# Expert weights in 8 KB pieces per partition, tokens transposed by strided reads, and padded tile addresses

## The chip, the core and the metric

The kernel runs on one core of a Trainium2 chip. Its metric is device time in microseconds (us), from the first to the last instruction, including what the launch adds. The engines are TensorE (PE, with its weight loads shown apart as PEld), VectorE (DVE), ScalarE (ACT), GpSimd (POOL) and SyncE (SP, which here issues nearly all loads). SBUF has 128 partitions; a tile is a number of bytes at the same address in every partition.

## What is computed

Two transformer blocks follow one another on 1024 tokens of 1024 features, all in float32. The first mixes tokens with a gated short convolution, the second with an mLSTM and a pooling group. Each ends in a mixture of experts, and only their expert weights are loaded differently by the change:

```
# block 1: 16 experts, each takes the 128 tokens that score highest for it
hid = silu(xs @ w_gate[e]) * (xs @ w_up[e])      # xs 128 x 1024, matrices 1024 x 1024
y[idx[e]] += (hid @ w_down[e]) * g[e]

# block 2: 32 experts, each token goes to its best 2, in blocks of tokens of one expert
a = xb @ w_gate[e]; b = xb @ w_up[e]             # 1024 x 512 each
out = (silu(a) * b) @ w_down[e]                  # 512 x 1024
```

The weights of one block's experts are 201 MB (16 x 12.6 MB, then 32 x 6.3 MB). They are read once.

## The kernel before, in words

**Loads.** Every weight matrix of an expert is cut along its rows into chunks of 1 MB: 256 rows of 1024 numbers, or 512 rows of 512. `chunk_src` (L750) gives a chunk's source. In chunk form a row number is k * 128 + p: partition p takes rows p, 128 + p, ... So a partition's 8 KB come as two pieces of 4 KB (block 1, and `w_down` of block 2) or four of 2 KB (`w_gate` and `w_up` of block 2), each from another place. The class `Loader` issues the chunks from SP in a fixed order (L92), one `raw` buffer each, never more than four in flight; some 14 to 15 buffers let it run ahead. 192 chunks belong to each block.

**Matmul in three products.** A number is split into a high and a low part (`split`, L190 to L192: ACT writes the high part, DVE the low one), and `mm3` (L199 to L201) adds three products. `hl` is the split weight chunk half, `xT` and `hT` the split, transposed tokens and hidden values. In the experts `xT` or `hT` is the stationary operand (the weight load of TensorE) and `hl` the moving one, 512 columns at a time. An expert of block 1 needs 3 matrices x 8 row blocks x 2 halves x 3 products = 144 such matmuls; a sub-block of 128 tokens of block 2 needs 72. In the projections of the two mixers, `hl` is stationary and `hT`, the tokens, moves.

**Transposes.** `gather` brings 128 token rows into `xg`. `Experts.transposed` (L522) turns them: feature block k, that is columns k * 128 to k * 128 + 127, becomes `xT[:, k]`, so that the partition of a feature is the partition in which its weight row lies. The token tile is the stationary operand, the identity moves. The hidden values `hid` are turned in the same way into `hT`. Where an expert of block 2 has few tokens (`SMALL`: 32 or 64), `transposed_few` (L532) does it, and the product is taken in plain float32 straight from `raw` (`product_few`, L551), without a split.

**Order.** Block 1 takes its 16 experts one after the other: gate, up, transposes of the next expert's tokens, down of the previous one. Block 2 does the same over 32 slots: full slots, four slots with two sub-blocks (5, 10, 15, 20), ten slots with 32 tokens, and six with 64 tokens at the end.

**Addresses.** Pools lay their tiles one behind the other, each rounded up to 32 bytes; pools of the right side grow downwards from the end. A tile that grows or shrinks therefore moves all that are laid behind it. Pool `h1` holds the tokens of the first mixer, with pool `hl1` behind it. Pool `c2` on the right holds small constants of block 2 (`block2_consts`), with `rawB1`, `rawC1` and `xhl1` (the `hl` tiles of block 1's experts) and later one half of `hT2` laid against it.

Of the kernel before, what the change touches and what calls it, by code (L numbers as in the profile page):

```python
# [12 lines left out]
F32 = mybir.dt.float32  # L13
# [8 lines left out]
P = 128  # L22
T = 1024
D = 1024
# [98 lines left out]
def kernel(ctx, tc, a, out):  # L123
    nc = tc.nc
# [7 lines left out]
    def sub_pool(stack, name, bufs=1, side=None):  # L132
        return stack.enter_context(tc.tile_pool(name=name, bufs=bufs, reuse_waits="tile", side=side))
# [8 lines left out]
    def mm_ps(kind="mm"):  # L142
        return banks[kind].tile([P, 2, 512], F32, tag=kind, name=kind)

    def aux_ps(n=512, kind="aux"):
        return banks[kind].tile([P, n], F32, tag=kind, name=kind)
# [18 lines left out]
    def col8(ap):  # L165
        return ap.rearrange("(k p) -> p k", p=P)
# [6 lines left out]
    ident = const.tile([P, P], F32, name="ident")  # L173
# [16 lines left out]
    def split(hl, raw, lo=nc.vector):  # L190
        nc.scalar.copy(hl[:, 0], raw)  # L191
        lo.tensor_tensor(hl[:, 1], raw, hl[:, 0].bitcast(F32), op=OP.subtract)  # L192

    def split_psum(hl, src):
        nc.scalar.copy(hl[:, 0], src)  # L195
        nc.vector.tensor_tensor(hl[:, 1], src, hl[:, 0].bitcast(F32), op=OP.subtract)  # L196
# [300 lines left out]
    class Experts:  # L497
# [19 lines left out]
        def scatter(self, y, idx, m=P):  # L517
            nc.gpsimd.indirect_dma_start(out=self.acc, out_offset=bass.IndirectOffsetOnAxis(ap=idx[:m], axis=0),  # L518
                                         in_=y[:m], in_offset=None, compute_op=OP.add,
                                         bounds_check=T - 1, oob_is_err=False)  # L520

        def transposed(self, x, n, tag):  # L522
            t = self.tile(tag, [2, n, P], self.wide, F32R)
            for q in range(n // 4):
                ps = aux_ps()
                for i in range(4):
                    k = q * 4 + i
                    nc.tensor.transpose(ps[:, i * P:(i + 1) * P], x[:, k * P:(k + 1) * P], ident)
                split_psum(t[:, :, q * 4:(q + 1) * 4].rearrange("p a b c -> p a (b c)"), ps)
            return t  # L530

        def transposed_few(self, x, n, tag, m):  # L532

            ps = aux_ps()
            for k in range(n):
                nc.tensor.transpose(ps[:, k * m:(k + 1) * m], x[:m, k * P:(k + 1) * P], ident[:m, :m])
            t = self.tile(tag, [2, n, P], self.wide)[:, 0, :, :m]
            nc.scalar.copy(t, ps[:, :n * m].rearrange("p (k c) -> p k c", k=n))
            return t
# [210 lines left out]
    def chunk_src(w, c, n):  # L750
        rows = slice(c * P * 2048 // n, (c + 1) * P * 2048 // n)
        if not isinstance(w, tuple):
            return w[rows, :].rearrange("(k p) f -> p k f", p=P)
        _, w3, i = w

        def src():
            if i not in dyn_ids:
                dyn_ids[i] = nc.values_load(slot_row[0][0:1, i:i + 1], engines=(mybir.EngineType.SP,),
                                            min_val=0, max_val=N_EXP2 - 1)
            return w3[bass.ds(dyn_ids[i], 1), rows, :].rearrange("o (k p) f -> p (o k) f", p=P)  # L760
        return src

    dyn_ids, slot_row = {}, {}

    def queue_experts(blocks):
        for i, kind in unit_order(len(blocks)):
            for key, w, c, _, n in blocks[i][kind] if kind in "gud" else ():
                ld.queue(key, [P, 2048 // n, n], chunk_src(w, c, n))
# [7 lines left out]
    def block1():  # L776
        x = a["x"][0]
# [6 lines left out]
        hp = sub_pool(s2, "h1")  # L784
        hT = [hp.tile([P, 2, KC, 512], F32R, name=f"hT{i}") for i in range(2)]
        gcol = hp.tile([P, KC], F32, name="gcol")
        cw = hp.tile([P, 3, KC], F32, name="cw")
        bcol = hp.tile([P, 2, KC], F32, name="bcol")
        sr = s1.enter_context(ExitStack())
        adap = sub_pool(sr, "adap", side="right")  # L790
        ada = Ada(adap, (sub_pool(sr, "adaraw", bufs=3, side="right"), 3))
# [35 lines left out]
        ps = {}  # L827
# [99 lines left out]
        def after_wo0():  # L927
            sr.close()
            block2_consts()
            more_raw(sw, "rawB1", 4)  # L930
# [127 lines left out]
    Q = {}  # L1058

    def block2_consts():  # L1060
        w_in = a["w_in_2"][0]
        sq = ctx.enter_context(ExitStack())
        pool = sub_pool(sq, "c2", side="right")
        Q["stack"] = sq

        def tl(name, shape, src):
            Q[name] = pool.tile(shape, F32, name="q_" + name)
            nc.sync.dma_start(Q[name], src)
            return Q[name]

        gcol = tl("gcol", [P, KC], col8(a["norm1_g_2"][0]))
        for i, m in ((0, 1), (1, 0)):
            nc.sync.dma_start(acol[:, 1, i], col8(mod_d[6 + m]))
        tl("convw", [P, 4, 4], a["conv_w_2"][0].rearrange("t (k p) -> p t k", p=P))
        for name, src in (("convb", "conv_b_2"), ("mng", "mlstm_norm_g_2"), ("msk", "mlstm_skip_2"), ("pb", "b_pool_2"),
                          ("psc", "pool_scale_2")):
            tl(name, [P, 4], col8(a[src][0]))
        bif = Q["bif"] = pool.tile([8, 1], F32, name="q_bif")
        nc.sync.dma_start(bif[0:4], a["b_igate_2"][0].rearrange("(h o) -> h o", o=1))
        nc.sync.dma_start(bif[4:8], a["b_fgate_2"][0].rearrange("(h o) -> h o", o=1))  # L1080
        tl("wif", [P, KC, 8], w_in[:, 1536:1544].rearrange("(k p) f -> p k f", p=P))

        tri = Q["tri"] = pool.tile([P, P], F32, name="q_tri")
        nc.gpsimd.affine_select(tri, ones, pattern=[[1, P]], compare_op=OP.is_ge, fill=0.0, base=0, channel_multiplier=-1)

        corr = Q["corr"] = pool.tile([P, 4, 16], F32, name="q_corr")
        for g in range(4):
            nc.gpsimd.tensor_scalar(corr[:, g], C["io"][:, 0:16], 1.0, float(2 << g), op0=OP.add, op1=OP.min)

        def finish():  # L1090
            nc.vector.scalar_tensor_tensor(acol[:, 1, 0], acol[:, 1, 0], 1.0, gcol, op0=OP.add, op1=OP.mult)
            nc.vector.tensor_tensor(Q["pb"], Q["pb"], Q["psc"], op=OP.mult)
            nc.vector.reciprocal(corr, corr)
        Q["finish"] = finish
# [844 lines left out]
    def extra_block(ex, pool, hlp, i, lists, wg, wu, wd):  # L1939

        ids, gates, row = lists
        e = nc.values_load(row[0:1, bass.ds(i, 1)], engines=(mybir.EngineType.SP,), min_val=0, max_val=N_EXP2 - 1)
        idx = pool.tile([P, 1], I32, tag="xidx", name="xidx", bufs=1)
        nc.vector.tensor_copy(idx, ids[:, bass.ds(i, 1)])
        gate = pool.tile([P, 1], F32, tag="xgate", name="xgate", bufs=1)
        nc.vector.tensor_copy(gate, gates[:, bass.ds(i, 1)])
        xT = ex.transposed(ex.gather(idx), KC, "xT")

        def load(w, h, kg):
            raw = pool.tile([P, 2048], F32, tag="xraw", name="xraw", bufs=2).rearrange("p (a b) -> p a b", a=4)  # L1950
            nc.sync.dma_start(raw, w[bass.ds(e, 1), kg * 512:(kg + 1) * 512, h * 512:(h + 1) * 512]
                              .rearrange("o (k p) f -> p (o k) f", p=P))
            hl = hlp.tile([P, 2, 4, 512], F32R, tag="hl", name="hl")
            split(hl, raw)
            return hl

        pg, pu, pd = mm_ps(), mm_ps(), mm_ps()
        for w, ps in ((wg, pg), (wu, pu)):
            for kg in range(2):
                ex.product(xT, load(w, 0, kg), ps[:, 0], range(kg * 4, kg * 4 + 4), 7)  # L1960
        hid = ex.tile("hid", [512], ex.wide)
        nc.scalar.activation(hid, pg[:, 0], AF.Silu)
        nc.vector.tensor_tensor(hid, pu[:, 0], hid, op=OP.mult)
        hT = ex.transposed(hid, 4, "hT")
        for h in range(2):
            ex.product(hT, load(wd, h, 0), pd[:, h], range(4), 3)
        y = ex.tile("yo", [D], ex.wide)
        nc.vector.scalar_tensor_tensor(y, pd.rearrange("p a b -> p (a b)"), gate, ex.grow, op0=OP.mult, op1=OP.mult)
        ex.scatter(y, idx)

    ps_stack = ctx.enter_context(ExitStack())
    routing_consts()
    block1()
    block2(acc_d[0])

# [27 lines left out]
```

## Time and profile before

| | us |
|---|---|
| median of 3 runs (2109.68 to 2112.94) | 2111.61 |
| the profiled execution, its own time | 2113.6 |
| span of that execution, first to last instruction | 2111.6 |
| PE busy in the span | 1908.3 |
| DVE busy | 1506.1 |
| ACT busy | 1035.9 |

The profile gives for each engine how long it was busy, in the span and in 40 slices of 53 us. Slices 9 to 19 (480 to 1010 us) are the experts of block 1, the last ten or so (from 1530 us) those of block 2. Matmuls are pipelined: a row shows 0.39 us for a matmul that begins 0.23 us after the one before, so the pace is read from the starts, not from the durations. DMA share is the mean busy share of 16 DMA engines; it can show a little over 1 since packets overlap.

### The profile page before, as it was taken

What the parts mean: (1) busy time and instruction counts of PE and PEld (TensorE: products, weight loads), DVE (VectorE), ACT (ScalarE), POOL (GpSimd) and SP (SyncE); (2) the same over time, 40 slices, a digit from 0 to 9 for tenths busy, and PEclk for the clock granted to TensorE, in tenths of its full rate; (3) what the DMA queues carried; (4) which work ended last, traced back from release to release, by engine and by line L of the source; (5) the groups of instructions that cost most, each with busy time, mean ns of one, the idle gap of its engine ahead of it and who ended that gap; (6) DMA issues with size and microseconds to landing.
All of it is one profiled execution on the core that took longest, in us unless ns stands there. A gap on an engine that the chain in (4) does not pass through costs nothing. (4 is left out here: it accounts for less than half of the span.)

```text
span 2111.6 us, 25403 instructions
## 1 busy us (share of the span) xinstructions
PE 1908.3 (90%) x9192; PEld 1477.3 (70%) x9192; DVE 1506.1 (71%) x1934; ACT 1035.9 (49%) x1454; POOL 334.8 (16%) x300
## 2 busy tenths in 40 slices
PE   4999999949999999999879999898799889898776
PEld 3788888837888888888757787687687667675222
DVE  6699975557999999999834367676896758676214
ACT  4311123216777777777654244332575646464113
POOL 1045430032010101000110000101411211211100
PEclk7999999969999999999979999999799999999988
DMA  9467746288999999999432011426899999999997
GB/s 319 144 234 260 257 145 226 104 292 309 378 377 394 382 393 380 394 373 381 124 106 80 11 35 36 160 110 242 303 391 296 380 358 369 373 371 355 360 368 298
DMA packets 235516, 573.56 MB, mean 272 GB/s; under 512 B 30311, under 2 KB 53575, under 8 KB 235388
## 3 DMA queue, kind: packets, MB, share of 16 engines
q1 hardware_dynamic: 215836, 511.78, 65.7%
q0 software_dynamic: 19168, 59.46, 9.8%
q8 instruction: 73, 1.20, 0.2%
q10 hardware_dynamic: 384, 0.68, 0.1%
q14 instruction: 55, 0.45, 0.1%
HBM read 534.12 MB, written 42.66 MB: 273 GB/s over the span
## 5 line engine op out<-in xcount | busy, mean ns | idle before, releaser
L192 DVE TENSOR_TENSOR hl<-raw,hl 128x1024 fp32r<-128x1024 f32 x601 | 721.9, 1234 | 149.6 <-ACT hl L191 145.2
L191 ACT CAST hl<-raw 128x1024 fp32r<-128x1024 f32 x612 | 634.5, 1053 | 287.8 <-PE mm L201 240.7
L199 PE MATMUL mm<-hl,xT 128*128 128x512 f32 x832 | 335.2, 403 | 0.3 <-ACT xT L195 0.3
L201 PE MATMUL mm<-hl,xT 128*128 128x512 f32 x832 | 331.1, 398 | 0.0
L200 PE MATMUL mm<-hl,xT 128*128 128x512 f32 x832 | 331.1, 398 | 0.0
L199 PE MATMUL mm<-hT,hl 128*128 128x512 f32 x448 | 180.8, 404 | 8.2 <-ACT hT L872 5.9
L201 PEld LDWEIGHTS mm<-hl,xT 128*128 128x128 f32 x832 | 158.7, 191 | 37.5 <-DVE xT L196 0.7
L199 PEld LDWEIGHTS mm<-hl,xT 128*128 128x128 f32 x832 | 159.2, 191 | 36.3 <-ACT xT L195 0.8
L200 PEld LDWEIGHTS mm<-hl,xT 128*128 128x128 f32 x832 | 159.2, 191 | 35.5
L200 PE MATMUL mm<-hT,hl 128*128 128x512 f32 x448 | 179.1, 400 | 1.6 <-DVE hT L873 1.6
L201 PE MATMUL mm<-hT,hl 128*128 128x512 f32 x448 | 176.7, 395 | 0.0
L199 PE MATMUL mm<-hl,hT 128*128 128x512 f32 x416 | 166.5, 400 | 0.2 <-ACT hT L195 0.2
L201 PE MATMUL mm<-hl,hT 128*128 128x512 f32 x416 | 163.8, 394 | 0.9 <-DVE hT L196 0.9
L200 PE MATMUL mm<-hl,hT 128*128 128x512 f32 x416 | 163.6, 393 | 0.0
L551 PE MATMUL mm<-raw,xT 128*32 128x512 f32 (+1 forms) x512 | 90.9, 642 | 29.4 <-DMA raw<-in_w_expert_up_dram 29.4
L199 PEld LDWEIGHTS mm<-hT,hl 128*128 128x128 f32 x448 | 85.6, 191 | 28.4 <-ACT hT L872 6.4
L301 DVE SCALAR_TENSOR_TENSOR adacc<-adaw,ccol,adacc 128x512 f32<-128x512 f32 x142 | 100.1, 771 | 0.3 <-DMA adaw<-in_ada_w_dram 0.3
L200 PEld LDWEIGHTS mm<-hT,hl 128*128 128x128 f32 x448 | 85.8, 191 | 19.7 <-DVE hT L873 2.8
L201 PEld LDWEIGHTS mm<-hT,hl 128*128 128x128 f32 x448 | 85.6, 191 | 19.3
L518 POOL DMA_INDIRECT acc_d<-yo,idx x35 | 54.7, 1562 | 274.8 <-DVE yo L736 123.2
L201 PEld LDWEIGHTS mm<-hl,hT 128*128 128x128 f32 x416 | 78.1, 188 | 19.4 <-DVE hT L196 1.4
L199 PEld LDWEIGHTS mm<-hl,hT 128*128 128x128 f32 x416 | 78.1, 188 | 17.4 <-ACT hT L195 0.5
(485 smaller groups left out, 2933.6 us busy)
## 6 DMA issues: line engine op xcount, KB each, us to landing
raw<-in_moe_w_gate_dram SPq DMA_DIRECT2D x64, 1024.0 KB
raw<-in_moe_w_up_dram SPq DMA_DIRECT2D x64, 1024.0 KB
raw<-in_moe_w_down_dram SPq DMA_DIRECT2D x64, 1024.0 KB
raw<-in_w_expert_gate_dram SPq DMA_DIRECT2D x64, 1024.0 KB
raw<-in_w_expert_down_dram SPq DMA_DIRECT2D x63, 1024.0 KB
raw<-in_w_expert_up_dram SPq DMA_DIRECT2D x62, 1024.0 KB
adaw<-in_ada_w_dram SPq DMA_DIRECT2D x47, 1024.0 KB
raw<-in_sc_w_in_dram SPq DMA_DIRECT2D x9, 1024.0 KB
```

The costliest lines, as they stand in the source:

```text
L191: nc.scalar.copy(hl[:, 0], raw)
L192: lo.tensor_tensor(hl[:, 1], raw, hl[:, 0].bitcast(F32), op=OP.subtract)
L199: nc.tensor.matmul(o, s_hi, m_hi, start=start, stop=False)
L200: nc.tensor.matmul(o, s_hi, m_lo, start=False, stop=False)
L201: nc.tensor.matmul(o, s_lo, m_hi, start=False, stop=stop)
L301: nc.vector.scalar_tensor_tensor(acc[kk % 2], w[:, k], c, add, op0=OP.mult, op1=OP.add)
L518: nc.gpsimd.indirect_dma_start(out=self.acc, out_offset=bass.IndirectOffsetOnAxis(ap=idx[:m], axis=0), in_=y[:m], in_offset=None, compute_ ...
L551: nc.tensor.matmul(ps[at:at + m], sT[:, k], w, start=k < split, stop=k > last - split)
```

## The change

Three things change together.

- The row number in a chunk becomes p * k: partition p takes 2 adjoining rows of 1024 numbers or 4 adjoining rows of 512, which is one piece of 8 KB. The bytes of a chunk, the chunks and their order stay.
- A feature must lie in the partition of its weight row. So the transposes take every second column (`q = 2`: all of block 1, and `hid` of block 2) or every fourth column (`q = 4`: the tokens of block 2) instead of 128 adjoining ones; `block` gives that view. Everything else about them stays.
- A tile `h1_pad` of 64 bytes stands behind the tokens of the first mixer, five tiles of 16 bytes (each rounded to 32) become one of 80 bytes, and `q_pad` of 32 bytes is added. That moves `hl1` by 64 bytes, and `rawB1`, `rawC1`, `xhl1` and the second half of `hT2` by 32.

In the built programs the pairs of operands that meet in TensorE lie at these addresses, given as the remainder by 256 (a chunk, a row block or a buffer of the same tile is a multiple of 256 away):

| stage | one operand | the other | before | after |
|---|---|---|---|---|
| projections of mixer 1 | `hT0`, `hT1` (87008, 119776) | `hl` of `hl1` (152736, then 152800) | 224, 160 | 224, 224 |
| experts of block 1 | `xT` (82912), `hT` (58336) | `hl` of `xhl1` (96960, then 96992) | 224, 192 | 224, 224 |
| mixer 2, tokens 0 to 511 | `hT2` (89664) | `hl` (128576) | 64, 64 | 64, 64 |
| mixer 2, tokens 512 to 1023 | `hT2` (195264, then 195296) | `hl` (128576) | 192, 64 | 224, 64 |
| output of mixer 2, first half | `wo` (195264, then 195296) | `yl` (132032) | 192, 192 | 224, 192 |
| experts of block 2 | `xT` (62432), `hT` (87008) | `hl` of `xhl2` (106464) | 224, 224 | 224, 224 |

The instructions of all engines stand in the same order as before. The loop for more tokens than the slots hold (`extra_block`) loads in two pieces where it loaded in one; with these inputs it runs no round.

```
+        def block(self, x, k, tag):
+            q = 2048 // (D if tag == "hT" else self.fdim)
+            return x.rearrange("t (c p q) -> t c q p", p=P, q=q)[:, k // q, k % q]
...
-                    nc.tensor.transpose(ps[:, i * P:(i + 1) * P], x[:, k * P:(k + 1) * P], ident)
+                    nc.tensor.transpose(ps[:, i * P:(i + 1) * P], self.block(x, k, tag), ident)
...
-                nc.tensor.transpose(ps[:, k * m:(k + 1) * m], x[:m, k * P:(k + 1) * P], ident[:m, :m])
+                nc.tensor.transpose(ps[:, k * m:(k + 1) * m], self.block(x[:m], k, tag), ident[:m, :m])
...
-            return w[rows, :].rearrange("(k p) f -> p k f", p=P)
+            return w[rows, :].rearrange("(p k) f -> p k f", p=P)
...
-            return w3[bass.ds(dyn_ids[i], 1), rows, :].rearrange("o (k p) f -> p (o k) f", p=P)
+            return w3[bass.ds(dyn_ids[i], 1), rows, :].rearrange("o (p k) f -> p (o k) f", p=P)
...
+        hp.tile([P, 16], F32, name="h1_pad")
...
-        for name, src in (("convb", "conv_b_2"), ("mng", "mlstm_norm_g_2"), ("msk", "mlstm_skip_2"), ("pb", "b_pool_2"),
-                          ("psc", "pool_scale_2")):
-            tl(name, [P, 4], col8(a[src][0]))
+        vecs = pool.tile([P, 5, 4], F32, name="q_vecs")
+        for i, (name, src) in enumerate((("convb", "conv_b_2"), ("mng", "mlstm_norm_g_2"), ("msk", "mlstm_skip_2"),
+                                         ("pb", "b_pool_2"), ("psc", "pool_scale_2"))):
+            Q[name] = vecs[:, i]
+            nc.sync.dma_start(Q[name], col8(a[src][0]))
+        pool.tile([P, 8], F32, name="q_pad")
...
-            nc.sync.dma_start(raw, w[bass.ds(e, 1), kg * 512:(kg + 1) * 512, h * 512:(h + 1) * 512]
-                              .rearrange("o (k p) f -> p (o k) f", p=P))
+            q = 2048 // w.shape[2]
+            for i in range(4 // q):
+                rows = slice(kg * 512 + i * q * P, kg * 512 + (i + 1) * q * P)
+                nc.sync.dma_start(raw[:, i * q:(i + 1) * q], w[bass.ds(e, 1), rows, h * 512:(h + 1) * 512]
+                                  .rearrange("o (p k) f -> p (o k) f", p=P))
```

## Rows read from the trace of the kernel before

**Rows 1.** The page: TensorE's and DMA's busy tenths in 40 slices.

```profile
PE   4999999949999999999879999898799889898776
...
DMA  9467746288999999999432011426899999999997
```

**Rows 2.** Busy time by stage: us, PE, PEld, DVE, ACT, POOL, clock, DMA share, GB/s.

```profile
528.00:1003.00 475.00, 475.00 (x2155) 386.00 (x2154) 443.03 (x405) 372.15 (x390) 41.34 (x33) 1.00 1.02 383
1637.00:2059.00 422.00, 365.07 (x1902) 240.15 (x1896) 237.06 (x249) 188.77 (x249) 68.13 (x53) 0.94 1.03 367
```

**Rows 3.** Waits of SP's queue, 540 to 1000 us, longest row: total us, times, longest.

```profile
SPq L92 <- DVE hl L192: 226.9, 132, 4.2
```

**Rows 4.** Waits of SP's queue, 1637 to 2071 us, longest row.

```profile
SPq L92 <- DMA raw<-in_w_expert_up_dram: 117.1, 45, 5.0
```

**Rows 5.** PE's timeline, block 1 experts, an unbroken run of 95: start, us, instruction.

```profile
579.93 0.39 PE L200 MATMUL mm<-hl,xT 128*128 128x512 f32 x1
...
601.86 0.39 PE L201 MATMUL mm<-hl,xT 128*128 128x512 f32 x1
```

**Rows 6.** PE's timeline, block 2 experts, an unbroken run of 47.

```profile
1534.27 0.40 PE L200 MATMUL mm<-hl,xT 128*128 128x512 f32 x1
...
1544.73 0.39 PE L201 MATMUL mm<-hl,xT 128*128 128x512 f32 x1
```

**Rows 7.** PE's timeline, projections of mixer 1, an unbroken run of 1007.

```profile
90.08 0.39 PE L200 MATMUL mm<-hT,hl 128*128 128x512 f32 x1
...
320.35 0.39 PE L201 MATMUL mm<-hT,hl 128*128 128x512 f32 x1
```

**Rows 8.** PE's timeline, mixer 2: 23 over tokens 512 to 1023, then 23 over 0 to 511.

```profile
1211.78 0.39 PE L200 MATMUL half<-hT,hl 128*128 128x512 f32 x1
...
1216.89 0.39 PE L201 MATMUL half<-hT,hl 128*128 128x512 f32 x1
...
1218.24 0.39 PE L200 MATMUL half<-hT,hl 128*128 128x512 f32 x1
...
1223.26 0.39 PE L201 MATMUL half<-hT,hl 128*128 128x512 f32 x1
```

**Rows 9.** DMA packets of 662.5 to 678.2 us (4 KB pieces), and 1730.4 to 1736.1 (2 KB).

```profile
DMA packets 1668, 6.46 MB, mean 411 GB/s; under 512 B 95, under 2 KB 95, under 8 KB 1667
...
DMA packets 1113, 2.21 MB, mean 387 GB/s; under 512 B 35, under 2 KB 35, under 8 KB 1113
```

**Rows 10.** DMA loads issued, 1633 to 2071 us, and the queue's packets, MB, share.

```profile
q1 hardware_dynamic: 61209, 145.17, 89.7%
...
raw<-in_w_expert_down_dram SPq DMA_DIRECT2D x48, 1024.0 KB
raw<-in_w_expert_up_dram SPq DMA_DIRECT2D x46, 1024.0 KB
raw<-in_w_expert_gate_dram SPq DMA_DIRECT2D x44, 1024.0 KB
```

**Rows 11.** The same queue, 540 to 1000 us.

```profile
q1 hardware_dynamic: 42544, 164.05, 90.5%
```

**Rows 12.** PE's timeline: eight transposes of 128 columns, and eight of 32.

```profile
566.76 1.04 PE L528 MATMUL aux<-ident,xg 128*128 128x128 f32 x8
...
1611.75 0.68 PE L536 MATMUL aux<-ident,xg 32*128 32x32 f32 x8
```

**Rows 13.** Single transposes by line: min/median/max ns, first and last start.

```profile
L528 PE MATMUL aux<-ident,xg x8: 272/272/273, 566.8 to 567.5; 128*128 128x128 f32 x8
...
L536 PE MATMUL aux<-ident,xg x56: 220/221/243, 1707.5 to 1945.8; 32*128 32x32 f32 x56
```

**Rows 14.** Single lines of DVE: min/median/max ns; L1013 reads at steps of 1 to 2.

```profile
L1013 DVE TENSOR_TENSOR mg<-mg x14: 211/216/219, 455.5 to 462.3; 64x64 f32<-64x64 f32 x7, 32x64 f32<-32x64 f32 x7
...
L968 DVE TENSOR_REDUCE mx<-af x1: 286/286/286, 437.6 to 437.6; 128x8 f32<-128x128 f32 x1
...
L1047 DVE TENSOR_REDUCE sl<-at x1: 366/366/366, 470.3 to 470.3; 128x16 f32<-128x128 f32 x1
```

## Prediction

> **What bounds the kernel now.** I read the 40 slices of the page first: where is TensorE full, and where is the DMA full? [rows 1] TensorE is at 9 tenths or more from slice 2 on, with dips near 430, 1080 and 1450 us, where routing is worked out, and sinks to 8 and 7 tenths at the end. The DMA is full twice, in the experts of block 1 and in those of block 2. The busy times by stage part these two cases [rows 2]. In block 1 (528 to 1003 us) PE is busy for all of 475 us at full clock: TensorE sets the pace. The DMA share of 1.02 beside it looks like a second bound, so the third view is what the load queue waits for: above all a `raw` buffer that the split has not yet emptied, 226.9 us of waiting [rows 3]. Loads are ahead; they are paid for by nobody.
>
> In block 2 this turns round. Between 1637 and 2059 us PE is busy 365 of 422 us [rows 2], and the load queue now waits for its own earlier loads: 117.1 us for those of `w_up`, and two more rows like it for `w_down` and `w_gate` [rows 4]; with four in flight, each new load starts when one lands. Loads set the pace from 1633 us to the end.
>
> So two things can shorten the kernel: the pace of a matmul up to 1003 us, and the time of a load after 1633 us. The change touches both.
>
> **The pads: pace of the matmuls.** A row of a matmul says 0.39 us everywhere; the pace is the distance of starts. Block 1's experts: 94 steps in 21.93 us, 233.3 ns each [rows 5]. Block 2's experts run the same instruction on the same shapes at 46 steps in 10.46 us, 227.4 ns [rows 6]. Both are at the full granted clock of 2.4 GHz. What differs is where the tiles lie. The table of addresses in the section on the change gives the remainders by 256: equal (224, 224) in block 2, 32 apart in block 1. Three other stages let me test that reading. Projections of mixer 1, 64 apart: 230.27 us / 1006 = 228.9 ns [rows 7]. Mixer 2 uses one tile of each half of the tokens in turn: 128 apart 232.3 ns, equal 228.2 ns [rows 8]. So equal remainders go with the fast pace in every stage, and 32 and 128 apart with the slow one. This is a correlation of one trace, no proof, but the two halves of mixer 2 differ in little else.
>
> The change makes the remainders equal in block 1 and in mixer 1. Block 1: 16 experts x 144 = 2304 matmuls x 5.9 ns = 13.6 us. Mixer 1: 24 units x 48 = 1152 x 1.5 ns = 1.7 us. Block 1 keeps PE busy without a gap [rows 2] and so does mixer 1, with 1007 matmuls in one run [rows 7], so this is on the path. In mixer 2 the second half goes from 128 to 160 apart, which no row prices; it stays slow, I take 0. The first half of mixer 2's output goes from 0 to 32 apart: 8 tiles x 24 = 192 x 5.9 = 1.1 us lost. Pads together: 14.2 us gained.
>
> Can the other engines follow? DVE is busy 443 of 475 us in block 1 [rows 2], so 33.0 us of an expert's 35.3; at the new pace of 34.5 it still fits. The loads must come 2.6% faster; they have been waiting for buffers, and 11 to 15 of them are ahead at the start. Neither is late next by these rows.
>
> **The 8 KB pieces: time of a load.** For the price of a piece I looked for stretches with full queues and no gathers. With 4 KB pieces, 15.7 us hold 1573 pieces (the rest are tiny): 15.7 x 16 / 1573 = 159.7 ns a piece on one engine. With 2 KB pieces, 5.7 us hold 1078: 84.6 ns [rows 9]. The second 2 KB of a piece therefore cost 75.1 ns and about 9.5 ns are paid per piece. An 8 KB piece, which no expert load shows, is extrapolated to 159.7 + 150.2 = 309.9 ns. A load of 1 MB is 64 KB on each engine: 32 x 84.6 = 2.71 us, 16 x 159.7 = 2.56 us, 8 x 309.9 = 2.48 us. So a gate or up load of block 2 gains 0.228 us, a down load 0.076 us. From 1633 us 90 gate and up loads and 48 down loads are issued [rows 10]: 20.5 + 3.6 = 24.1 us. TensorE follows: it is idle 57 of 422 us [rows 2], 13.5%, where loads get shorter by 0.175 of 3.17 us (438 us by 138), 5.5%. In block 1 the loads gain too, and nothing comes of it but slack.
>
> Bounds: if pieces beyond 4 KB gain nothing more, 90 x 0.152 = 13.7 us. Upwards, fit share x 16 x time = a x packets + b x bytes to the two whole stretches [rows 10, 11]: 6285 and 6661 engine-us give a = 16.6 ns. That price contains the crowding by gathers and scatters; by it the gain is 90 x 24 x 16.6 + 48 x 8 x 16.6 = 42 us. I take 24.1, from clean stretches.
>
> A page prices the same thing lower. The Trainium skill (DMA: Bandwidth & Descriptors, section Why small descriptors are slow) has about 3 DMA cycles of fixed cost per packet, 3.5 ns at that page's 850 MHz. An estimate by it: 24 pieces fewer x 3.5 ns on 90 loads and 8 fewer on 48 are 8.9 us, and the time would be 2088 us. The measured 9.5 ns speaks against it.
>
> **The strided transposes.** 256 transposes of block 1 read every second number, the tokens of block 2 every fourth; they are weight loads in float32, and no weight load of this trace has a step. Eight transposes take 1.04 us [rows 12], one 0.27 [rows 13], so one follows the other after (1.04 - 0.27) / 7 = 110 ns. With only 32 columns moving, the same weight load of 128 columns recurs every (0.68 - 0.22) / 7 = 66 ns [rows 12, 13]. So the weight load has some 44 ns of cover. What does a step cost? DVE reads 64 numbers adjoining in the first pass of L1013 and every second one in the last, and all 14 take 211 to 219 ns. A reduction over a step of 16 numbers takes 366 ns where the same count adjoining takes 286 [rows 14]: 80 ns. I take nothing for step 2 (the DVE row at that very step), and 80 ns for step 4: 66 + 80 = 146, 36 ns over today's pace, some 6 us in all of block 2, hidden in TensorE's idle time there. If step 2 also paid 80 ns, block 1 lost 256 x 36 = 9 us. A gain has no reason.
>
> **The sum.** 2113.6 (the profiled execution, span 2111.6) - 14.2 - 24.1 = 2075.3 us. It lies 2.0 us over the median of the runs, so 2073 us is the median forecast.
>
> **The rivals.** First, only half of it does what it says. *Pieces over 4 KB gain nothing:* 2111.6 - 14.2 - 13.7 = 2084 us. Any limit between DMA and memory at the 411 GB/s of the 4 KB stretch would do that; against it, those packets still show a fixed part. *The pads do nothing:* the slow pace is not the address but the company, since block 1 has ACT and DVE busier than block 2. Then 2111.6 - 24.1 = 2087 us. Mixer 2's two halves speak against it.
>
> Second, slower: *strided weight loads stall TensorE.* If each number of a stepped read costs what four adjoining ones cost, a weight load takes 4 x 66 = 264 ns instead of 110. In block 1, 256 x 154 = 39 us, all on the path. In block 2, 240 transposes of 128 columns x 154 = 37 us and 192 of the small slots x 198 = 38 us meet an idle time of 57 us that shrinks by the 24 us: 75 - 33 = 42 us come out. 2073 + 39 + 42 = 2154 us. It decides from about 150 ns in block 1 alone, or 80 to 100 ns with block 2. For it: no row excludes it on TensorE. Against it: DVE pays 80 ns at a much wider step, of which 44 are covered. The Trainium skill (SBUF — State Buffer, section Door 1) says that SBUF is read in lines of 16 bytes and that at least two hits per line are needed for full speed. By that rule step 2 is free and step 4 pays, which leaves the sum as it is and makes this rival less likely; no run here has shown it.
>
> **How the numbers follow.** Forecast as summed, 2060 to 2083: 0.60. Pieces gain nothing beyond 4 KB, or as little as the page says: 0.17, 2084 to 2088. Pads do nothing: 0.11, 2087. Strides stall: 0.07, around 2154 and slower than before in most of it. The rest, 0.05: something eats the gains (a memory that likes 8 KB pieces less), 0.03 of it within 0.2%, which is about what a measurement of this kernel can tell from no change, and 0.02 slower. Range: down to 2055 (42 us for the loads), up to 2098 (both half rivals at once, 2111.6 - 13.7); outside lie the stall, the rest and some way beyond either bound, under 0.2. Faster 0.89, same 0.03, slower 0.08.
>
> **What would show it.** The page's packets fall by 24,576 + 49,152 + 8,192 = 81,920; more, and pieces are cut on the way. Clean stretches of block 2 show about 423 GB/s instead of 387. The steps of `mm<-hl,xT` in block 1 fall to 227 ns; block 1 ends 15 us earlier. `L528` keeps 110 ns between transposes in block 1 and shows up to 146 on the tokens of block 2. In block 2 loads are issued every 3.0 us, still waiting for loads. The forecast is wrong if TensorE shows new gaps behind the transposes, or if loads wait for buffers from 1633 us on, for then TensorE has become the bound.

## The result: 2095.1 us, and the profile after

| | us |
|---|---|
| before, median (2109.68 to 2112.94) | 2112.2 |
| after, median (2094.06 to 2096.56) | 2095.1 |
| ratio, 95% interval | 0.9922 (0.9904 to 0.9939) |
| forecast | 2073 |

The change gains 17 us where 38 were forecast. The way is right, the time lies in the range near its upper end, and less than half of the gain came. Two questions follow: which part gave the 17 us, and where did the other 21 go?

The same views as ahead of the prediction, now of the changed kernel. First the page: TensorE's and the DMA's busy tenths in 40 slices (compare [rows 1]), and the packets.

```profile
PE   4999999949999999999789999898799898898986
...
DMA  9467746288999999999422001426798989999998
DMA packets 154108, 573.56 MB, mean 274 GB/s; under 512 B 30311, under 2 KB 53575, under 8 KB 104828
```

The packets fell from 235,516 on the page of before by 81,408, where 81,920 were forecast. New are dips in the DMA's row near its end: a 7 that was 8, and twice an 8 that was 9. Next, busy time by stage (us, PE, PEld, DVE, ACT, POOL, clock, DMA share, GB/s), to be read against [rows 2].

```profile
528.00:1003.00 475.00, 475.00 (x2194) 396.82 (x2193) 448.71 (x413) 380.64 (x399) 42.88 (x34) 1.00 0.99 385
1637.00:2059.00 422.00, 379.98 (x1922) 254.05 (x1924) 236.81 (x249) 186.69 (x246) 67.22 (x53) 0.95 0.98 369
```

In the same 422 us of block 2 TensorE is now busy 380 us instead of 365 (some 11 of these 15 us are the stepped transposes, as an experiment below shows), and the DMA share has fallen under 1. The loads have gone from 367 to 369 GB/s, nearly nothing. The load queue says why (engine, line, what it waited for: us, times, longest), to be read against [rows 4]; the first fence is the row on buffers of before's list, 1637 to 2071 us, the second is after's list, 1620 to 2050 us.

```profile
SPq L92 <- DVE hl L192: 12.4, 9, 4.3
```

```profile
SPq L92 <- DMA raw<-in_w_expert_down_dram: 94.6, 37, 4.7
SPq L92 <- DMA raw<-in_w_expert_up_dram: 81.6, 37, 4.9
SPq L92 <- DVE hl L192: 79.1, 33, 4.9
SPq L92 <- DMA raw<-in_w_expert_gate_dram: 76.6, 37, 3.8
SPq L92 <- PE mm L556: 11.7, 11, 3.9
```

Before, loads waited for loads, and for buffers only 12.4 us. Now they wait 79.1 us for a buffer that a split has still to read and 11.7 us for one that a small slot's product reads (L556). So the loads are faster, and then stand still. Where? Around the double slots, the only ones with two sub-blocks of 128 tokens. Stretches of 20 us there, before and then after (columns as above):

```profile
1600.00:1620.00 20.00, 20.00 (x105) 15.79 (x107) 12.56 (x12) 11.09 (x14) 1.07 (x1) 1.00 0.73 238
...
1680.00:1700.00 20.00, 20.00 (x92) 16.53 (x91) 13.75 (x13) 11.75 (x14) 2.52 (x2) 1.00 1.04 370
...
1880.00:1900.00 20.00, 20.00 (x94) 16.37 (x93) 10.82 (x10) 9.78 (x12) 1.04 (x1) 1.00 1.04 369
```

```profile
1680.00:1700.00 20.00, 20.00 (x92) 16.46 (x91) 9.80 (x9) 8.34 (x10) 0.81 (x1) 1.00 0.71 256
...
1880.00:1900.00 20.00, 20.00 (x99) 16.48 (x101) 12.09 (x12) 10.10 (x12) 1.04 (x1) 1.00 0.77 283
```

TensorE is full in both kernels. Before, the DMA was full beside it (1.04) from the second double slot on: a tie. After, it falls to 0.71 and 0.77 (and to 0.86 in the stretch between, 1780 to 1800 us): the buffers are all taken, and loads wait until TensorE gets on. At the first double slot, 1600 to 1620 us, the trace of before shows the same at 0.73: what becomes of loads that are ahead could be read there ahead of the change.

Two other lines of the profile confirm steps of the prediction. In block 1 an unbroken run of 95 matmuls now takes 21.35 us, 227.1 ns a step, against 233.3 [rows 5] (start, duration, instruction):

```profile
574.78 0.40 PE L200 MATMUL mm<-hl,xT 128*128 128x512 f32 x1
...
596.13 0.40 PE L201 MATMUL mm<-hl,xT 128*128 128x512 f32 x1
```

And three clean stretches of 8 KB pieces, one in block 1 (656.9 to 671.2 us) and two in block 2 (1985.4 to 1994.2, 2041 to 2051.2), run at 422 to 424 GB/s, against 411 and 387 of [rows 9]:

```profile
DMA packets 833, 6.04 MB, mean 422 GB/s; under 512 B 97, under 2 KB 97, under 8 KB 97
...
DMA packets 513, 3.71 MB, mean 422 GB/s; under 512 B 60, under 2 KB 60, under 8 KB 60
...
DMA packets 594, 4.33 MB, mean 424 GB/s; under 512 B 67, under 2 KB 67, under 8 KB 67
```

One line went against the forecast: the transposes. Eight of 128 columns take 1.11 us instead of 1.04, eight of 32 columns 1.14 instead of 0.68 [rows 12].

```profile
561.71 1.11 PE L533 MATMUL aux<-ident,xg 128*128 128x128 f32 x8
...
1598.84 1.14 PE L541 MATMUL aux<-ident,xg 32*128 32x32 f32 x8
```

### The profile page after: what moved, and what is told of

Same layout as the page of the kernel before. It is cut to its first block, busy times and chain, and to the rows that moved or that the text cites. A ratio compares the mean times of both kernels' runs of the same rounds, so it can differ in the third digit from the quotient of the medians.

```text
span 2094.0 us, 25405 instructions
## 1 busy us (share of the span) xinstructions
PE 1903.0 (91%) x9192; PEld 1494.4 (71%) x9192; DVE 1502.5 (72%) x1934; ACT 1036.3 (49%) x1454; POOL 332.4 (16%) x300
## 4 chain that ended last, share of the span: by engine, by line
PE 64%; DMA 13%; issue 11%; DVE 7%; ACT 2%; POOL 2%; DVEq 0%; POOLq 0%; SPq 0%; ACTq 0%
PE mm L201 17%; PE mm L199 17%; PE mm L200 17%; DMA raw<-in_w_expert_up_dram 4%; DMA acc_d<-yo,idx 4%; DMA raw<-in_w_expert_down_dram 2%; PE aux L533 2%; PE half L201 1%; PE half L199 1%; PE half L200 1%; PE aux L417 1%; PE aux L1595 1%; POOL acc_d L518 1%; DVE hl L192 1%; POOL xg L512 1%
## 5 line engine op out<-in xcount | busy, mean ns | idle before, releaser
L199 PE MATMUL mm<-hl,xT 128*128 128x512 f32 x832 | 331.1, 398 | 0.2 <-ACT xT L195 0.2
L200 PE MATMUL mm<-hl,xT 128*128 128x512 f32 x832 | 327.7, 394 | 0.0
L201 PE MATMUL mm<-hl,xT 128*128 128x512 f32 x832 | 327.7, 394 | 0.0
L556 PE MATMUL mm<-raw,xT 128*32 128x512 f32 (+1 forms) x512 | 85.8, 621 | 16.3 <-DMA raw<-in_w_expert_up_dram 16.3
L201 PEld LDWEIGHTS mm<-hT,hl 128*128 128x128 f32 x448 | 85.3, 190 | 18.1
```

Source lines behind the costliest of these rows:

```text
L199: nc.tensor.matmul(o, s_hi, m_hi, start=start, stop=False)
L200: nc.tensor.matmul(o, s_hi, m_lo, start=False, stop=False)
L201: nc.tensor.matmul(o, s_lo, m_hi, start=False, stop=stop)
L556: nc.tensor.matmul(ps[at:at + m], sT[:, k], w, start=k < split, stop=k > last - split)
```

## The experiments

The runs were made in several sets, and the kernel before came out between 2111.5 and 2113.8 us in them (2111.5 with the first four experiments, 2113.8 with the matmuls left out, 2112.6 with the new order of slots). A difference of 1 or 2 us between runs of two sets means nothing.

**Theory.** Pads: as forecast. Pieces: a load is as fast as forecast, but block 2 is bound in turns, by TensorE in full and double slots and by loads in small ones; the buffers can't carry the gain across. Steps: they cost TensorE time in block 2, part of it on the path. **Rivals:** the pads alone did all (pieces and steps are worth nothing); the steps alone ate the gain of the loads; loads beside gathers and scatters are no faster.

### The parts one by one

**The pads alone**, on the kernel before.

```
+        hp.tile([P, 16], F32, name="h1_pad")
...
+        vecs = pool.tile([P, 5, 4], F32, name="q_vecs")
+        pool.tile([P, 8], F32, name="q_pad")
```

> The kernel before with the address pads alone: old pieces, adjoining transposes. If equal address remainders set the pace of a matmul, block 1's experts step at 227 ns (233.3 before) and mixer 1's at 227 (228.9 before), and the time is 2112 - 13.6 - 1.7 + 1.1 = 2098 us. If the pace of block 1 came from the company of ACT and DVE, it stays at 233 and the time at 2112.

Measured: 2096.5 us, ratio 0.9928 (0.9912 to 0.9945). The address theory holds; 15 of the 17 us are the pads.

**The changed kernel without the pads** (the same lines taken out again).

> The changed kernel without the pads: 8 KB pieces and stepped transposes. If pads and pieces add up, 2095 + 15 = 2110 us, that is, pieces and steps together are worth only 2 us. If the pads give less together with the pieces than alone, 2100 or less.

Measured: 2108.4 us, 0.9986 (0.9976 to 0.9996). Pads and the rest add up within 1 us: pieces and steps together are worth 3.1 us, and with the 15.0 of the pads that makes 18.1 against the 17.1 of the change.

**Pieces without steps in block 2.**

```
         def block(self, x, k, tag):
+            if self.fdim == 512:
+                return x[:, k * P:(k + 1) * P]
```

> The changed kernel, but in block 2 the transposes read 128 adjoining columns again, so features meet wrong weight rows there (same bytes, same work; block 1 is unchanged). Theory of turns: loads and TensorE bind block 2 in turns, the steps cost TensorE some 58 ns in each of 192 small transposes and 11 ns in 240 large ones, about 14 us, and part of it is on the path: 2083 to 2090 us. Rival, the steps alone ate the gain of the loads: 2077 us, 24 us under the pads alone but for 3 us of steps in block 1. Rival, steps are hidden: 2095 us as the changed kernel.

Measured: 2091.8 us (2091.1 to 2092.5), 0.9901 (0.9884 to 0.9917). The steps of block 2 cost 3.3 us, a little less than the theory wanted (2083 to 2090 us). The rival that they ate the gain falls: without them 2077 us should have come.

**Steps without pieces in block 2**: the kernel before with the pads, and `block` in the transposes of block 2 alone.

> The kernel before with the pads and, in block 2 alone, the stepped transposes of the change on the old pieces (features meet wrong weight rows there; same bytes, same work). The price of the steps where loads bind: theory of turns, 1 to 6 us over the pads alone, since most of the 14 us falls into TensorE's waits for loads. Rival, steps cost in full: 14 us over the pads alone.

Measured: 2098.6 us, 0.9937 (0.9921 to 0.9954), 2.0 us over the pads alone, hardly beyond the scatter of the runs. From 1637 to 2059 us TensorE is busy 376.53 us against 365.37 with the pads alone:

```profile
1637.00:2059.00 422.00, 376.53 (x1901) 251.48 (x1901) 232.12 (x242) 185.11 (x244) 66.11 (x51) 0.95 1.03 366
```

```profile
1637.00:2059.00 422.00, 365.37 (x1902) 237.49 (x1902) 231.54 (x242) 184.03 (x242) 64.51 (x51) 0.94 1.04 367
```

Some 11 us more work, of which 2 come out. From these four, with 2.7 us for the steps of block 1 (256 transposes, each 9 to 11 ns later; below), the pieces in block 2 are worth 2096.5 - 2091.8 + 2.7 = 7.4 us, not 24.1.

Where in block 2 do pieces and steps come out? The timelines of the four profiled executions tell. Column one is the time from the first product of the first double slot to that of the fourth, column two from there to the last product of the slots of 64 tokens.

| all with the pads | double slot 1 to 4, us | from there to the last product, us |
|---|---|---|
| pads alone | 284.6 | 207.5 |
| and steps in block 2 | 288.4 | 205.1 |
| and pieces, no steps in block 2 | 289.1 | 193.7 |
| the changed kernel | 293.4 | 194.4 |

The faster loads shorten only the end, by 11 to 14 us. Between the double slots block 2 gets longer with them, by 4.5 to 5 us, and the steps there come out by some 4 us with either pieces. Why longer, is in the waits. These are TensorE's in the kernel before, 1637 to 2059 us:

```profile
PE mm L551 <- DMA raw<-in_w_expert_up_dram: 26.0, 9, 7.0
PE aux L536 <- DVE xT L196: 24.1, 4, 6.7
```

So TensorE's idle 57 us are two things. The 26.0 us for loads all lie behind 1950 us, in the last slots. The 24.1 us lie behind the four pairs of slots with 32 tokens, and no load ends them. There VectorE waits for a tile `yo`, in which a small slot keeps its up product; the tile is free when a scatter of an earlier result has read it (`acc_d<-yo,idx`), and TensorE waits behind VectorE. Both waits with the pads alone (1572 to 1930 us), then with pieces and no steps (1577 to 1930 us):

```profile
PE aux L536 <- DVE xT L196: 23.7, 4, 6.6
DVE yo L565 <- DMA acc_d<-yo,idx: 18.3, 4, 5.0
```

```profile
PE aux L543 <- DVE xT L196: 29.7, 4, 8.1
DVE yo L572 <- DMA acc_d<-yo,idx: 24.3, 4, 6.5
```

Beside 8 KB pieces the scatters hold VectorE 6 us longer. Three of the four waits lie between the double slots: 1.5 us each, the 4.5 us of the table. With the steps on the old pieces the wait of VectorE stays short (17.0 us in four waits, 1573 to 1930 us). So in the slots of 32 tokens the theory is wrong: what TensorE waits for there is no load. That another tile for the up product would save these waits was not tested.

### Is it TensorE that keeps the loads' gain?

The test: make TensorE short in block 2's experts, so that nothing but loads can bind, in both kernels with pads.

```
+                if self.fdim == 512:
+                    nc.tensor.matmul(ps, sT[:, 0, k], hl[:, 0, i], start=k == 0, stop=k == last)
+                    continue
                 mm3(ps, sT[:, 0, k], sT[:, 1, k], hl[:, 0, i], hl[:, 1, i], k == 0, k == last)
```

> The kernel before with the pads; in block 2's experts only the first of the three products is computed in the slots with a split (two of three matmuls are left out there), so that TensorE can't bind block 2 and loads alone do. It is the base for the next run: loads of 2 and 4 KB pieces. I expect 2098 minus little, 2080 to 2098 us, and the load queue waiting for its own loads all through block 2.

> The changed kernel with the same two matmuls of three left out in block 2's experts. If faster loads are a full gain where nothing but loads binds, it lies under the run before by 110 gate and up loads x 0.228 + 55 down loads x 0.076 = 29 us, less 3 us for the steps in block 1. If the loads of 8 KB pieces aren't faster beside gathers and scatters, the two are within 5 us.

Measured, two runs each: 2092.3 us with the old pieces, 2069.0 with the new ones, 23.3 us apart where 26 were expected. TensorE is busy 261 and 280 of 430 us (1620 to 2050) although its granted clock falls to 0.78 and 0.80 there. With the old pieces, TensorE's work is nearly free to leave out: 4 us, or 6 by the ratios to each set's kernel before. With the new ones it is worth 2095.1 - 2069.0 = 26 us. The load queue with the new pieces, 1620 to 2030 us, waits for buffers no more:

```profile
SPq L92 <- DMA raw<-in_w_expert_down_dram: 115.5, 44, 4.3
SPq L92 <- DMA raw<-in_w_expert_up_dram: 104.7, 45, 4.6
SPq L92 <- DMA raw<-in_w_expert_gate_dram: 98.2, 44, 4.0
SPq L92 <- DVE hl L192: 1.8, 6, 0.4
```

So the loads gain nearly what was forecast, beside gathers and scatters too, and TensorE, with what it waits for in the slots ahead of the last ones, keeps the gain from coming out. The rival that loads aren't faster there falls.

If that is so, the order of the slots must matter with the new pieces and not with the old. Small slots (as many loads as the others, for less work of TensorE) are put between full and double ones, so that fewer buffers fill:

```
-PAIRS_AT = (5, 10, 15, 20)
-HALF_AT = (26, 27, 28, 29, 30, 31)
-QUARTER_AT = (6,7,11,12,16,17,21,22,25,24)
+PAIRS_AT = (5, 9, 14, 20)
+HALF_AT = (19, 25, 27, 29, 30, 31)
+QUARTER_AT = (3, 4, 6, 7, 10, 11, 15, 16, 21, 22)
```

> The changed kernel with block 2's slots in another order: the slots of 32 and 64 tokens, where loads bind, are spread between the full and the double slots, where TensorE binds (double slots at 5, 9, 14, 20; 32 tokens at 3, 4, 6, 7, 10, 11, 15, 16, 21, 22; 64 tokens at 19, 25, 27, 29, 30, 31). Theory of turns: the buffers fill at fewer double slots, the load queue waits less for buffers, and part of the missing 20 us comes back: 2075 to 2088 us. If the buffers aren't what holds the loads, 2095 us as before.

> The kernel before with the pads and the same new order of slots. There the loads bind nearly all of block 2, so the order should be worth little: 2092 to 2097 us (2096.5 with the old order). If the order itself is worth as much here as with the 8 KB pieces, the run before says nothing about buffers.

Measured: on the changed kernel 2087.7 us (2082.8 to 2091.2), 0.9875 (0.9858 to 0.9892), 7.4 us less than with the old order. On the kernel before with the pads 2098.3 us (2097.3 to 2099.2), 1.8 more and 1 over what was expected: there the order gains nothing. So its worth hangs on the pieces, as the theory says. The number of buffers itself was not varied. The rest is not all back: in the reordered changed kernel loads still wait for buffers, 54.3 us, against 79.1:

```profile
SPq L92 <- DVE hl L192: 54.3, 21, 4.9
```

### What does a step cost, and where?

One kernel, run once, holds two measurements: steps of 1, 2, 4, 8 from slot to slot in block 2 (`t (c p q) -> t c q p` with that q), and other addresses (`h1_pad` of 32 bytes; `q_vecs` without `q_pad`). Its time says nothing.

> A measurement on the kernel before, in one look. The transposes of block 2 read at steps of 1, 2, 4 and 8 numbers in turn, slot by slot (features meet wrong weight rows in block 2, same bytes and same work). And other tile addresses: mixer 1 32 apart (64 before), block 1 32 apart on the other side (remainders 0 and 224), the second half of mixer 2 64 apart (0 and 64; 128 before). If the address sets the pace: mixer 1 slows from 228.9 to 233 ns a step, block 1 stays at 233, the second half of mixer 2 goes from 232 to 229. If the pace is a matter of what runs beside, all stay as before: 229, 233, 232. Small transposes: 62 ns at step 1 and 120 at 2 and 4; at step 8 120 if any step costs one price, more if lines of memory count.

Measured, the steps: eight small transposes at step 1 (L525), 2 (L527), 4 (L529) and 8 (L531).

```profile
1627.56 0.68 PE L525 MATMUL aux<-ident,xg 32*128 32x32 f32 x8
...
1712.64 1.14 PE L527 MATMUL aux<-ident,xg 32*128 32x32 f32 x8
...
1723.85 1.14 PE L529 MATMUL aux<-ident,xg 32*128 32x32 f32 x8
...
1616.42 1.06 PE L531 MATMUL aux<-ident,xg 32*128 32x32 f32 x8
```

The median distance of the starts of single ones is 62 ns at step 1, 120 at step 2 and at step 4 alike, and 110 at step 8. That refutes both of my guesses: step 2 isn't free on TensorE, and step 4 costs no more than it. For transposes of 128 columns, whose 109 ns cover nearly all of that, it is 120 against 109 ns.

Measured, the addresses. Mixer 1, 32 apart, 1007 matmuls (88.92 to 323.65 us); mixer 2, second half with the tokens moving (remainders 0 and 64), 23 matmuls; its V projection with the tokens stationary (64 and 0), 23 matmuls.

```profile
88.92 0.39 PE L200 MATMUL mm<-hT,hl 128*128 128x512 f32 x1
...
323.65 0.39 PE L201 MATMUL mm<-hT,hl 128*128 128x512 f32 x1
```

```profile
1165.24 0.39 PE L200 MATMUL mm<-wv,hT 128*128 128x512 f32 x1
...
1170.29 0.40 PE L201 MATMUL mm<-wv,hT 128*128 128x512 f32 x1
...
1216.31 0.40 PE L200 MATMUL half<-hT,hl 128*128 128x512 f32 x1
...
1221.44 0.40 PE L201 MATMUL half<-hT,hl 128*128 128x512 f32 x1
```

Mixer 1: 234.73 us / 1006 = 233.3 ns, against 228.9 before [rows 7]: moving a tile by 32 bytes slows a stage in which nothing else changed. Block 1, now 32 apart on the other side, stays at 233.3 ns (mean of the starts). With the run of the pads alone that settles the rival of the company. One expectation failed: 64 apart isn't always 229 ns. With the moving operand 64 ahead (V projection) it is 5.05 us / 22 = 229.5; with the stationary one 64 ahead (second half of mixer 2) 5.13 us / 22 = 233.2.

### Taking the steps away

The tokens and the hidden values can be written in the order of the weight rows, so that transposes read adjoining columns; the step then lies in the reads of the instructions that write them.

```
-                nc.scalar.activation(h2, xr, AF.Copy, scale=ss[:, 0:1])
+                nc.scalar.activation(flatq(h2), mixq(xr), AF.Copy, scale=ss[:, 0:1])
...
-                    nc.scalar.activation(s["hid"], p, AF.Silu)
+                    nc.scalar.activation(ex.flat(s["hid"]), ex.mixed(p), AF.Silu)
```

Here `mixed` reads `t (s q) -> t q s`, and `flat` writes adjoining.

> The changed kernel without stepped transposes: the tokens and the hidden values are written in the order of the weight rows (column f goes to the place of f mod q, then f / q), so every transpose reads 128 adjoining columns, and the step lies in the reads of the ACT, DVE and POOL instructions that write. Transposes should follow each other at 109 and 62 ns again; 2.7 us in block 1 and the 3.3 us of block 2 that adjoining transposes were worth: 2089 us. If steps cost those engines as much as they cost TensorE and it shows, 2093 to 2096.

Measured: 2095.1 us (2091.8 to 2096.2), 0.9919 (0.9903 to 0.9936): no gain in the median, though the transposes are fast again and block 1 gains what was expected. The starts of two successive groups of transposes of tokens are one expert apart: 35.33 us before, 34.65 after, 34.46 here (the two fences are after and this kernel).

```profile
527.06 1.11 PE L533 MATMUL aux<-ident,xg 128*128 128x128 f32 x8
```

```profile
527.34 1.03 PE L548 MATMUL aux<-ident,xg 128*128 128x128 f32 x8
...
561.80 1.03 PE L548 MATMUL aux<-ident,xg 128*128 128x128 f32 x8
```

With 561.71 (shown above) after's distance is 34.65. The steps of block 1 cost (34.65 - 34.46) x 16 = 3 us (2.7 as counted). What stands against it: the writers of block 2's tokens. Rows by line (min/median/max ns): DVE's, at step 2 in block 1, then at step 4 in block 2, and ACT's and POOL's of block 2's last tile; below, ACT and POOL in the changed kernel.

```profile
L500 DVE SCALAR_TENSOR_TENSOR h<-xr,ss,arow x14: 743/749/755, 337.2 to 418.1; 128x512 f32<-128x512 f32 x14
...
L500 DVE SCALAR_TENSOR_TENSOR h<-xr,ss,arow x14: 1129/1140/1156, 1353.1 to 1444.4; 128x512 f32<-128x512 f32 x14
...
L491 ACT ACTIVATE h<-xr,ss x1: 2117/2117/2117, 1455.7 to 1455.7; 128x1024 f32<-128x1024 f32 x1
...
L492 POOL TENSOR_TENSOR h<-h,arow x1: 2845/2845/2845, 1457.9 to 1457.9; 128x1024 f32<-128x1024 f32 x1
```

```profile
L483 ACT ACTIVATE h<-xr,ss x1: 1148/1148/1148, 1454.8 to 1454.8; 128x1024 f32<-128x1024 f32 x1
...
L484 POOL TENSOR_TENSOR h<-h,arow x1: 2333/2333/2333, 1456.0 to 1456.0; 128x1024 f32<-128x1024 f32 x1
```

Step 2 is free on DVE (749 ns against 748 adjoining) and costs ACT 66 ns and POOL 30 in block 1's last tile (1214 against 1148, 2372 against 2342); step 4 costs DVE 392 ns on 512 numbers, ACT 969 and POOL 512 on 1024. The last tile's chain, ACT and two POOL steps, is 2 us longer; DVE's 14 writes of this row take 5.5 us more, and the 14 additions behind them as much again. Against the changed kernel, this one is 2.7 us ahead at the end of block 1's experts and 2.1 us behind when block 2's are under way. That these writes alone caused those 5 us was not tested apart. Nor do they settle the whole: the profiled execution is the fastest of the four (2091.8 us), and it ends 4 us ahead of the changed kernel's, so block 2's experts gained 6 us in it.

**The parts that pay, together.** New order of slots; block 1's tokens and all hidden values written in order (step 2); block 2's tokens turned with step 4 as in the change; `yl` moved by 32 bytes, which makes the output of mixer 2 equal by 256 again.

> The changed kernel with the new order of slots, with block 1's tokens and all hidden values written in the order of the weight rows (the reads of step 2 that cost ACT and DVE nothing in the run with all values written in order), block 2's tokens turned with step 4 as in the change, and yl and wo of mixer 2 equal by 256. From 2088 us for the slots: 2.7 less in block 1, 1 less in mixer 2, 1 to 2 less in block 2: 2082 to 2084 us. If adjoining transposes are worth nothing in block 2 it is 2084; if the time of block 2 scatters as with the new order alone, the interval is some 4 us wide.

Measured: 2082.0 us (2077.2 to 2088.3, 5 runs), 0.9861 (0.9842 to 0.988): the fastest kernel that leaves nothing out, 13 us under the changed kernel and 30 under the kernel before. **With block 2's tokens written in order as well**, at step 4:

> All together: 8 KB pieces, pads, values written in order, slots in the new order, and a pad of 32 bytes that makes yl and wo of mixer 2's output equal by 256 again (1.1 us). The parts summed: 2095 - 6 - 1 - what the order of slots gives (7 to 20) = 2068 to 2081 us.

Measured: 2090.7 us (2088.1 to 2091.2), 0.9897 (0.9881 to 0.9914), a miss: 10 us over the upper end of what the summed parts promised, and 9 over the version that leaves block 2's tokens to the transposes. Why is open. The dearer writes of step 4 show as 4.4 us at block 2's first product (1486.4 us, against 1482.0 without them), but at the first double slot the two profiled executions are level (1560.8 and 1561.4), and they part behind it, to 2056.4 and 2048.8 us at the last product.

## Why the prediction was right and wrong, point by point

- **What bounds the kernel.** Right for block 1. For block 2 half right: leaving out two thirds of the split matmuls gained only 4 to 6 us with the old pieces, so loads did bind. What I didn't read is how near TensorE was: 20.00 of 20 us busy at the double slots, beside a DMA at 1.04, and no wait for a load from 1640 to 1950 us. "Loads set the pace from 1633 us to the end" holds for TensorE only in the last slots.
- **Pads, 14.2 us.** Right: 15.0 us measured alone. The pace in block 1 is 227.1 ns, in mixer 1 228.09 us / 1006 = 226.7 ns (an unbroken run from 90.13 to 318.22 us).
- **Time of a load.** Right: 422 to 424 GB/s where 423 were extrapolated, and 23 us of gain where only loads bind. An estimate by the Trainium skill's fixed cost per packet (DMA: Bandwidth & Descriptors, section Why small descriptors are slow) gave 8.9 us for 138 loads; it is 10.8 us for the 165 loads of that test. The 23.3 us speak against it here.
- **Loads, 24.1 us on the path.** This is the step that failed: "TensorE follows: it is idle 57 of 422 us", a mean over the stage. In double slots there is no idle time, and loads that ran ahead stood still there for want of a buffer (79.1 us of waiting, 12.4 before). Of the 57 us only 26.0 were waits for loads, all in the last slots, and there the gain came out. 24.1 us were waits behind scatters, which no faster load shortens; beside 8 KB pieces they grew by 6 us. 7.4 us came out; the missing 16.7 are most of the error of 22.
- **Transposes, 0 us.** Wrong: 2.7 us in block 1 and 3.3 us in block 2. The DVE row at "that very step" doesn't hold for a weight load: step 2 costs TensorE as much as step 4. The price of step 4 was set at 146 ns and is 120. But the 6 us of the forecast count the 160 large transposes of tokens alone (36 ns each) and leave out the 192 small ones, which went from 62 to 120 ns: 11 us. And the idle time that was to hide them was no spare time between the double slots.
- **The sum with measured terms:** 15.0 + 7.4 - 2.7 - 3.3 = 16.4 us, against 17.1 measured. That is no test: the 7.4 and the 3.3 are differences to the same run, so the sum must come out. The test is the run without the pads (18.1 against 17.1).
- **The rivals.** "Pieces over 4 KB gain nothing" (2084) was nearer in time, for a reason that is refuted: the pieces are faster. "Strides stall" priced the weight load at 264 ns; it is 120. The sentence that came true stood at the end: loads would wait for buffers from 1633 us on if TensorE became the bound. I had given that no chance and no price. That the time still lies in the range is luck: its upper end, 2098, was both half rivals at once, and neither holds.

Open: why the runs with the new order of slots scatter (2077 to 2091 us), what more buffers or a tile of its own for the up product would give, and why scatters land later beside 8 KB pieces.

## What to carry to other kernels

Before counting a faster transfer as time, look at the partner engine slice by slice, at the size of one work item: idle time counts only where it lies, and only if it is a wait for that transfer; ask of every gap what ended it. A change to one kind of transfer can also hold up another kind beside it. A tie between two engines is worth a test that makes one of them short, as leaving out matmuls did here: it shows what either is worth alone. Where operands lie in SBUF is worth a look when the same instruction has two paces in one kernel.

## What the runs showed of the hardware

- The pace of a float32r matmul of 512 columns depends on the remainders of the tiles' addresses by 256 bytes: 227 ns where moving and stationary operand have equal ones (up to 228.2 in mixer 2), 229 to 229.5 with the moving one 64 ahead, 232 to 234 at 32 apart on either side, at 64 the other way and at 128. That equality by 512 isn't needed shows in block 1 after: 96992 and 82912 are 55 x 256 apart, and the pace is 227.1 ns.
- A weight load of a transpose whose columns are not adjoining recurs after 120 ns at step 2 and 4 and some 110 at step 8, against 62 adjoining. The Trainium skill (SBUF — State Buffer, section Door 1) has 16-byte lines that want two hits each. DVE agrees (749 ns at step 2, 1140 at step 4, against 748), ACT and POOL nearly (step 2 costs 66 and 30 ns, step 4 969 and 512), TensorE's weight load does not.
- Pieces of 8 KB run at 422 to 424 GB/s, a gain over 4 KB (411) as large as the fixed cost of 9.5 ns per piece says.
- Beside loads in 8 KB pieces a scatter lands later: a median of 9.4 us from its issue (pieces, no steps) against 8.2 (pads alone), 1620 to 2050 us.
